# Last columns of an output projection: residual rows made one quarter of columns earlier, a part of the last norm on TensorE, the last block in 384 and 128 columns

## The chip, the cores and the metric

One core of a Trainium2 chip runs the whole kernel. The metric is device microseconds (us) of one execution; the figure quoted is the median of several executions.

## The reference, cut to what matters

Two layers over 512 latent tokens of 2048 features (and 256 context tokens, which only the first layer needs). The change touches the end of the second layer:

```
y_l   = sgu_mixer(xm_l, w_in_odd[j], ...)                 # 512 x 2048
x_lat = layer_norm(DEEPNORM_ALPHA * x_lat + g_l * (y_l @ w_out_odd[j]),
                   post_ln_g[layer], post_ln_b[layer])    # the output
```

`layer_norm` takes mean and variance over the 2048 features of a token, then multiplies by `post_ln_g` and adds `post_ln_b`. The `x_lat` on the right is the first layer's output. The kernel keeps it in DRAM without the first layer's factor and shift (`x1d`), so its residual rows are made when needed: `x1d * lng0 + lnb0`.

## The kernel before, in words

TensorE computes in fp32r, each operand split in a high and a low part: a product is three matmuls (high by high, high by low, low by high; lines 212 to 214). The parts of a weight are made by `split` (line 107): ScalarE casts the high part (L108), VectorE subtracts (L109).

The second output projection is one call of `out_phase` over four quarters of 512 columns, `out1`. In each quarter `form_b` runs over 16 blocks `kb` of the contraction, and for each over four blocks `t` of 128 tokens; the result of a `t` is one PSUM bank of 128x512. A quarter is 16 x 4 x 3 = 192 matmuls. The last quarter (c = 3) is called with `hold` = 16: token block t = 0 takes all 16 `kb` first, with the split weights kept in SBUF, then t = 1, 2 and 3 follow, each with 48 matmuls.

`evacuate` turns a finished bank into rows `z`: VectorE multiplies by the gate row (L1001), adds ALPHA times the residual rows (L1002) and takes statistics of the 512 columns (L1004). After the last quarter of a `t` the statistics are combined (L1051), EPS is added (L254), GpSimd takes the power -0.5 (L256), and `norm1` does, for each of four groups of 512 columns, a subtract-and-multiply (L1453), a multiply-and-add (L1454) and the DMA to `out` (L1455).

The residual rows: in the middle of a quarter (`n == KB // 2`) `ready` loads the two rows `lng0`, `lnb0`, broadcast to 128 partitions (L982, into a `pair_tile`), and the four 128x512 blocks of `x1d` (L1027, tag `t2`, four buffers). After that, one block per step, VectorE multiplies (L1033) and adds (L1034). The `pair_tile`s are four slots of 128x1024: slots 0 and 1 hold the gate rows of columns 0, 1 and 2, 3; slots 2 and 3 hold `lng0` and `lnb0` of even and of odd quarters.

The order of each engine's queue, the DMA issues on SyncE's queue included, is set when the kernel is built: a planner takes the program's instructions in order of priority (program order) as their inputs and buffers come free by its own times, so an instruction may stand ahead of its place in the text. `tc.issue_after(x)` puts the instructions in its block behind `x` on their engine. Everything then runs in that order.

Of the kernel before, what the change touches and what calls it, by code (L numbers as in the profile page):

```python
# [22 lines left out]
NH = 4  # L23
ALPHA = 4.0 ** 0.25
# [47 lines left out]
def tile_backbone(ctx: ExitStack, tc: tile.TileContext, io: dict, out: bass.AP):  # L72
    nc = tc.nc
    ve, sc, gp, te, dma = nc.vector, nc.scalar, nc.gpsimd, nc.tensor, nc.sync
    fl = Flow()

    big = ctx.enter_context(tc.tile_pool(name="big", bufs=1))
    wp = ctx.enter_context(tc.tile_pool(name="wp", bufs=1))
# [18 lines left out]
    ident = cst.tile([P, P], F32, tag="ident", name="ident")  # L97
# [45 lines left out]
    for c, _ in out1:  # L143
        stream += b_raws(io["woo"], c)
    raws, parts, used, newest, older = [], [], [0], [None], [None]


    AHEAD, HOLD = 2, 16
# [36 lines left out]
    def form_a(targets):  # L185

        for q in range(4):
# [13 lines left out]
                    te.matmul(pt[:, :n], b, xh_, start=False, stop=last)  # L201
            fl.pe(us)

    def form_b(tbs, stat, order, before=None, hold=0):


        pts = {t: ps() for t in tbs}
        ws = []

        def mm(t, n, kb, wh, wl):  # L210
            a, b = stat(kb, t)
            te.matmul(pts[t], a, wh, start=n == 0, stop=False)  # L212
            te.matmul(pts[t], a, wl, start=False, stop=False)  # L213
            te.matmul(pts[t], b, wh, start=False, stop=n == KB - 1)  # L214

        for n, kb in enumerate(order):
            if before is not None:
                before(n)
            ws.append(weights())
            now = tbs if n < KB - hold else tbs[:1]  # L220
            for t in now:
                mm(t, n, kb, *ws[n])
            fl.pe(3 * 0.216 * len(now))
        if not hold:
            yield pts
            return
        yield {tbs[0]: pts[tbs[0]]}
        for t in tbs[1:]:
            for n in range(KB - hold, KB):
                mm(t, n, order[n], *ws[n])  # L230
                fl.pe(3 * 0.216)
            yield {t: pts[t]}

    xh = [None] * KB
    xl = [None] * KB
# [61 lines left out]
    with ExitStack() as ev:  # L297
# [16 lines left out]
        rows = [[crow[k] for k in range(2)], [crows[:, k] for k in range(2)]]  # L314
# [32 lines left out]
        order = list(taken())  # L347
# [550 lines left out]
        for h in range(NH):  # L898
            qkv_tiles(h)
            ctx_in(h)  # L900
            early = h < 3
# [87 lines left out]

    def out_phase(seq, resid, gate, order, before, norm, finish, hold=0, affine=(), late=None):  # L990
        z = [la.tile([P, D], F32, tag=f"z{t}", name=nm("z")) for t in range(NT)]
        st = [la.tile([P, 4, 6], F32, tag=f"st{t}", name=nm("st")) for t in range(NT)]
        g = []

        evac, todo = [], []

        def evacuate(c, s, pts, xr):
            for n, t in enumerate(pts):
                if n and c < 3:
                    paced(z[t][:, s])  # L1000
                ve.tensor_tensor(z[t][:, s], pts[t], g[c], ALU.mult)  # L1001
                ve.scalar_tensor_tensor(z[t][:, s], xr[t], ALPHA, z[t][:, s], ALU.mult, ALU.add)  # L1002
                yield Y_E
                ve.bn_stats(st[t][:, c, :], z[t][:, s])  # L1004

        def product(c, tbs, before, hold, late):
            s = slice(c * 512, (c + 1) * 512)
            xr = {}

            def ready(n):  # L1010
                if before is not None:
                    before(n)
                if late is not None:
                    late(n)
                if n == KB // 2:
                    if not g:
                        gt = [pair_tile(i) for i in range(2)]
                        g.extend(half_row(gate, c_, gt[c_ // 2], c_ % 2) for c_ in range(4))
                    while evac:
                        fl.drain(evac.pop())  # L1020
                    rows = []
                    if affine:
                        rt = pair_tile(2 + c % 2)
                        rows = [half_row(a, c, rt, i) for i, a in enumerate(affine)]
                    for t in tbs:
                        xr[t] = la.tile([P, 512], F32, tag="t2", name=nm("xres"), bufs=4)
                        dma.dma_start(xr[t], resid[t * P:(t + 1) * P, s])  # L1027
                        if affine:
                            todo.append((xr[t], rows))
                if n > KB // 2 and todo:  # L1030

                    x_, rows = todo.pop(0)
                    ve.tensor_tensor(x_, x_, rows[0], ALU.mult)  # L1033
                    ve.tensor_tensor(x_, x_, rows[1], ALU.add)  # L1034

            for pts in form_b(tbs, y_stat, order, ready, hold):
                evac.append(fl.spawn(evacuate(c, s, pts, xr)))
                if c == 3:
                    fl.drain(evac.pop())
                yield pts  # L1040

        last = None
        for n, (c, tbs) in enumerate(seq):
            for pts in product(c, tbs, before if n == 0 else None, *((hold, late) if n == len(seq) - 1 else (0, None))):
                if c == 3:
                    if last is not None:
                        fl.drain(last)
                        last = None
                    for t in pts:
                        m2 = la.tile([P, 2], F32, tag="m2", name=nm("m2"), bufs=2)  # L1050
                        ve.bn_aggr(m2, st[t])  # L1051
# [59 lines left out]


    v = [None] * NT
    vst = [la.tile([P, 4, 6], F32, tag=f"st{t}", name=nm("vst")) for t in range(NT)]

# [218 lines left out]
    def spatial(q):  # L1334

        if q == 0:
            for t in range(NT):
                ve.bn_aggr(vm[t], vst[t])
# [234 lines left out]
```

## Time and profile before

| | |
|---|---|
| median of 3 runs | 1735.16 us (1733.09 to 1737.89) |
| the profiled execution | 1728.81 us, its span from first to last instruction 1726.9 us |
| mean granted TensorE clock | 0.997 of full speed |
| busy: TensorE, VectorE, ScalarE | 98%, 69%, 39% of the span |

How to read it: PE is the matmul side of TensorE and PEld its weight loads, DVE is VectorE, ACT ScalarE, POOL GpSimd, SP SyncE; SPq is SyncE's queue, which issues the DMAs. All places in time are us from the start of the span. A matmul's duration in a row contains the way through the array, so the pace of a stream is read from the distance of starts. Brackets at the end of a row give the idle time before it and what ended it.

### The profile page before, as it was taken

To read this page: it belongs to the slowest core of one execution; us is meant where nothing else is said; L and a number is where in the kernel's file an instruction comes from. 1 tells how busy PE (TensorE), PEld (TensorE's weight loads), DVE (VectorE), ACT (ScalarE), POOL (GpSimd) and SP (SyncE) were. 2 spreads that over 40 slices of the span, in tenths; PEclk is the share of its full clock that TensorE was granted. 3 is DMA by queue.
4 is the path that set the end of the run, shared out by engine and by line. 5 is a ranking of instruction groups with operands and counts; after the bars stand their busy time and mean duration, and the time that the engine had idled before them with its cause. 6 is when DMAs were issued, how large, how long until landed. Compare 5 with 4: busy or idle time off the path is not lost.

```text
span 1726.9 us, 22782 instructions
## 1 busy us (share of the span) xinstructions
PE 1700.4 (98%) x8260; PEld 1399.2 (81%) x8260; DVE 1200.2 (69%) x2133; ACT 681.8 (39%) x1176; POOL 75.1 (4%) x113
## 2 busy tenths in 40 slices
PE   8999999999999999999999999999999999999997
PEld 5777788888888888888888888877887888888885
DVE  5786486556798977866644477876876767665558
ACT  3223232323444445445432247634544354432230
POOL 0000000000000000000000000211110110000000
PEclk9999999999999999999999999999999999999998
DMA  8986277879687575663384567996767585765443
GB/s 316 375 333 254 83 244 241 278 268 316 226 279 273 202 250 173 213 197 123 111 261 138 147 225 263 214 275 168 217 166 221 134 242 137 208 168 166 131 143 113
DMA packets 143304, 366.63 MB, mean 212 GB/s; under 512 B 13526, under 2 KB 29870, under 8 KB 142678
## 3 DMA queue, kind: packets, MB, share of 16 engines
q1 hardware_dynamic: 127158, 324.79, 55.3%
q0 software_dynamic: 8640, 31.46, 10.3%
q10 hardware_dynamic: 7392, 8.91, 1.4%
q8 instruction: 65, 1.06, 0.2%
q14 instruction: 49, 0.40, 0.1%
HBM read 340.42 MB, written 24.69 MB: 211 GB/s over the span
## 4 chain that ended last, share of the span: by engine, by line
PE 96%; DMA 2%; DVE 1%; issue 0%; ACT 0%; DVEq 0%; SPq 0%; ACTq 0%
PE ps L212 11%; PE ps L214 11%; PE ps L213 11%; PE ps L1270 8%; PE ps L1271 8%; PE ps L1269 8%; PE ps L196 6%; PE ps L197 6%; PE ps L201 6%; PE ps L479 2%; PE ps L480 2%; PE ps L481 2%; PE ps L708 2%; DMA qr<-in_wq_dram 2%; PE ps L388 1%; PE ps L716 1%
## 5 line engine op out<-in xcount | busy, mean ns | idle before, releaser
L108 ACT CAST wh<-wr 128x512 fp32r<-128x512 f32 x328 | 201.1, 622 | 442.3 <-PE ps L214 260.9
L109 DVE TENSOR_TENSOR wh<-wr,wh 128x512 fp32r<-128x512 f32 x320 | 219.0, 687 | 202.0 <-ACT wh L108 200.3
L214 PE MATMUL ps<-wh,yl 128*128 128x512 f32 x512 | 199.5, 390 | 0.0
L212 PE MATMUL ps<-wh,yh 128*128 128x512 f32 x512 | 194.3, 391 | 0.0
L213 PE MATMUL ps<-wh,yh 128*128 128x512 f32 x480 | 187.0, 390 | 0.0
L196 PE MATMUL ps<-xh,wh 128*128 128x512 f32 x448 | 175.4, 392 | 0.0
L197 PE MATMUL ps<-xl,wh 128*128 128x512 f32 x448 | 175.0, 391 | 0.0
L201 PE MATMUL ps<-xh,wh 128*128 128x512 f32 x448 | 174.7, 390 | 0.0
L282 DVE SCALAR_TENSOR_TENSOR adw<-adw,crow 128x1024 f32<-128x1024 f32 x128 | 155.9, 1218 | 3.3 <-DMA adw<-in_adat_dram 3.3
L108 ACT CAST wh<-qr 128x1024 fp32r<-128x1024 f32 x96 | 101.1, 1058 | 138.0 <-DMA qr<-in_wq_dram 53.9
L1270 PE MATMUL ps<-wh,ch 128*128 128x512 f32 x384 | 149.8, 393 | 2.6 <-DVE wh L109 2.5
L1271 PE MATMUL ps<-wh,ch 128*128 128x512 f32 x384 | 149.0, 391 | 0.0
L1269 PE MATMUL ps<-wh,ch 128*128 128x512 f32 x384 | 143.5, 396 | 3.7 <-ACT wh L108 3.7
L109 DVE TENSOR_TENSOR wh<-qr,wh 128x1024 fp32r<-128x1024 f32 x96 | 116.6, 1221 | 28.9 <-PE ps L1270 12.8
L109 DVE TENSOR_TENSOR wh<-pair,wh 128x1024 fp32r<-128x1024 f32 x72 | 87.4, 1220 | 40.3 <-PE ps L1270 20.9
L1270 PE MATMUL ps<-wh,xn 128*128 128x512 f32 x288 | 112.6, 391 | 0.0
L1271 PE MATMUL ps<-wh,xn 128*128 128x512 f32 x288 | 112.5, 391 | 0.0
L214 PEld LDWEIGHTS ps<-wh,yl 128*128 128x128 f32 x512 | 96.1, 188 | 19.9
L212 PEld LDWEIGHTS ps<-wh,yh 128*128 128x128 f32 x512 | 96.0, 188 | 19.7
L1269 PE MATMUL ps<-wh,xn 128*128 128x512 f32 x288 | 107.6, 395 | 0.3 <-ACT wh L108 0.3
L213 PEld LDWEIGHTS ps<-wh,yh 128*128 128x128 f32 x480 | 90.2, 188 | 18.6
L108 ACT CAST wh<-pair 128x1024 fp32r<-128x1024 f32 x72 | 75.3, 1051 | 66.5 <-PE ps L1271 27.8
(320 smaller groups left out, 3281.5 us busy)
## 6 DMA issues: line engine op xcount, KB each, us to landing
adw<-in_adat_dram SPq DMA_DIRECT2D x128, 512.0 KB, 5.1
qr<-in_wq_dram SPq DMA_DIRECT2D x116, 512.0 KB, 4.8
wr<-in_wie_dram SPq DMA_DIRECT2D x60, 512.0 KB, 3.6
pair<-in_wq_dram POOLq DMA_DIRECT2D x56, 512.0 KB, 6.4
aw<-in_a_dram SPq DMA_DIRECT2D x52, 512.0 KB, 7.2
wr<-in_woe_dram SPq DMA_DIRECT2D x40, 512.0 KB, 4.5
wr<-in_woo_dram SPq DMA_DIRECT2D x32, 512.0 KB, 4.0
wr<-in_wv_dram SPq DMA_DIRECT2D x16, 512.0 KB, 5.4
```

Of the source, the lines that this page charges most:

```text
L108: sc.copy(hi, src)
L109: return ve.tensor_tensor(lo, src, f32(hi), ALU.subtract)
L196: te.matmul(pt[:, :n], a, xh_, start=first, stop=False)
L197: te.matmul(pt[:, :n], a, xl_, start=False, stop=False)
L201: te.matmul(pt[:, :n], b, xh_, start=False, stop=last)
L212: te.matmul(pts[t], a, wh, start=n == 0, stop=False)
L213: te.matmul(pts[t], a, wl, start=False, stop=False)
L214: te.matmul(pts[t], b, wh, start=False, stop=n == KB - 1)
L282: ve.scalar_tensor_tensor(ts[n], ts[n], 0.5, crow[k], ALU.mult, ALU.mult, accum_out=part[:, f % 4, k:k + 1])
L1269: te.matmul(pts[t], a, wh[:, s], start=first, stop=False, **more)
L1270: te.matmul(pts[t], a, wl[:, s], start=False, stop=False, **more)
L1271: te.matmul(pts[t], b, wh[:, s], start=False, stop=end, **more)
```

## The change

Three things, all in the second layer's last quarter of columns.

1. The residual rows of c = 3 are loaded and made in the third quarter (c = 2, from n = 13), into pair tiles 0 and 2, with `lng0`, `lnb0` in pair tile 3.
2. The last token block (t = 3) of c = 3 is computed as 384 and then 128 columns, each over all 16 `kb`, in two PSUM banks, and evacuated in these two parts (the statistics get a fifth group).
3. In the norm of t = 3, the multiply-and-add of the first 512 columns leaves VectorE: TensorE puts `lnb1` in a bank with a multiplication by the identity, adds diag(rstd) times the rows (plain fp32), and ScalarE copies the result back; ScalarE also makes diag(rstd). The four DMAs of t = 3 go out in the order 1, 2, 0, 3; for each `t` they stand behind its loop.

```
+    LAST = slice(0, 384), slice(384, 512)
     def form_b(tbs, stat, order, before=None, hold=0):
-        def mm(t, n, kb, wh, wl):
+        def mm(t, n, kb, wh, wl, s=slice(0, 512)):
             a, b = stat(kb, t)
...
+            te.matmul(pts[t][:, s], a, wh[:, s], start=n == 0, stop=False)
+            te.matmul(pts[t][:, s], a, wl[:, s], start=False, stop=False)
+            newest_mm[0] = te.matmul(pts[t][:, s], b, wh[:, s], start=False, stop=n == KB - 1)
...
         for t in tbs[1:]:
-            for n in range(KB - hold, KB):
-                mm(t, n, order[n], *ws[n])
-                fl.pe(3 * 0.216)
-            yield {t: pts[t]}
+            for s in (slice(0, 512),) if t != tbs[-1] else LAST:
+                if s.start:
+                    pts[t] = ps()
+                for n in range(KB):
+                    mm(t, n, order[n], *ws[n], s)
+                    fl.pe(3 * 0.000422 * (s.stop - s.start))
+                yield {t: pts[t]}
...
+        def evacuate(c, s, pts, xr, i=slice(0, 512)):
+            s = slice(s.start + i.start, s.start + i.stop)
...
+                ve.tensor_tensor(z[t][:, s], pts[t][:, i], g[c][:, i], ALU.mult)
+                ve.scalar_tensor_tensor(z[t][:, s], xr[t][:, i], ALPHA, z[t][:, s], ALU.mult, ALU.add)
                 yield Y_E
+                ve.bn_stats(st[t][:, n_st[t], :], z[t][:, s])
+                n_st[t] += 1
...
+                if hold and n == 0:
+                    xr.update(early)
+                if affine and c == 2 and n == KB - 3:
+                    rt, c_ = pair_tile(3), c + 1
+                    rows = [half_row(a, c_, rt, i) for i, a in enumerate(affine)]
+                    for i in (0, 2):
+                        x2 = pair_tile(i)
+                        for j in range(2):
+                            x_, t = x2[:, j * 512:(j + 1) * 512], i + j
+                            dma.dma_start(x_, resid[t * P:(t + 1) * P, c_ * 512:(c_ + 1) * 512])
+                            early[t] = x_
+                            todo.append((x_, rows))
-                if n == KB // 2:
+                if n == KB // 2 and hold:
+                    while evac:
+                        fl.drain(evac.pop())
+                elif n == KB // 2:
...
-                if n > KB // 2 and todo:
+                if (n > KB // 2 or hold) and todo:
...
     def norm1(t, z, m2, r_):
+        last = t == NT - 1
+        if last:
+            pt, dg = ps(), wp.tile([P, P], F32, tag="wraw", name="dg", bufs=3)
+            with tc.issue_after(newest_mm[0].ins):
+                te.matmul(pt, ident, lnr[1, 0], start=True, stop=False)
+            sc.activation(dg, ident, AF.Copy, scale=r_[:, 0:1])
         for c in range(4):
             s = slice(c * 512, (c + 1) * 512)
             ve.scalar_tensor_tensor(z[:, s], z[:, s], m2[:, 0:1], lnr[0, c], ALU.subtract, ALU.mult)
-            ve.scalar_tensor_tensor(z[:, s], z[:, s], r_[:, 0:1], lnr[1, c], ALU.mult, ALU.add)
+            if last and c == 0:
+                te.matmul(pt, dg, z[:, s], start=False, stop=True)
+                sc.copy(z[:, s], pt)
+            else:
+                ve.scalar_tensor_tensor(z[:, s], z[:, s], r_[:, 0:1], lnr[1, c], ALU.mult, ALU.add)
+        for c in (1, 2, 0, 3) if last else range(4):
+            s = slice(c * 512, (c + 1) * 512)
             dma.dma_start(out[t * P:(t + 1) * P, s], z[:, s])
```

## Rows read from the trace of the kernel before

**Rows 1.** The page: busy time of each engine with its share of the span, and the shares of the engines in the chain that ended last.

```profile
PE 1700.4 (98%) x8260; PEld 1399.2 (81%) x8260; DVE 1200.2 (69%) x2133; ACT 681.8 (39%) x1176; POOL 75.1 (4%) x113
...
PE 96%; DMA 2%; DVE 1%; issue 0%; ACT 0%; DVEq 0%; SPq 0%; ACTq 0%
```

**Rows 2.** Busy time by stretch: most of the third quarter of columns, then t = 0 and t = 3 of the last quarter. The columns are the stretch, its length, busy time of each engine (instructions), granted clock, share of the DMA engines, GB/s.

```profile
1640.00:1669.00 29.00, 29.00 (x129) 24.02 (x128) 13.32 (x21) 8.32 (x15) 0.00 (x0) 1.00 0.47 151
...
1671.40:1682.30 10.90, 10.90 (x50) 9.03 (x49) 8.54 (x18) 3.85 (x7) 0.00 (x0) 1.00 0.51 169
...
1704.10:1715.00 10.90, 10.85 (x48) 8.64 (x46) 10.09 (x18) 0.00 (x0) 0.92 (x1) 1.00 0.47 157
```

**Rows 3.** Instructions in order of time, PE, in t = 3 of the last quarter: two matmuls that stand 30 matmuls apart.

```profile
1707.31 0.39 PE L212 MATMUL ps<-wh,yh 128*128 128x512 f32 x1
...
1714.11 0.39 PE L212 MATMUL ps<-wh,yh 128*128 128x512 f32 x1
```

**Rows 4.** Instructions in order of time after TensorE's last matmul: DVE's (its L1002 and L1004 lie between the first two), and POOL's one.

```profile
1714.99 0.69 DVE L1001 TENSOR_TENSOR z<-ps,pair 128x512 f32<-128x512 f32 x1 [0.67 <-PE ps L214]
...
1717.17 0.26 DVE L1051 BATCH_NORM_AGGREGATE m<-st 128x2 f32<-128x24 f32 x1
1717.46 0.15 DVE L254 TENSOR_SCALAR vae<-m 128x1 f32<-128x1 f32 x1
1717.54 2.73 DVE L1453 SCALAR_TENSOR_TENSOR z<-z,m,lnr 128x512 f32<-128x512 f32 x4
1717.76 0.92 POOL L256 TENSOR_TENSOR rst<-vae,mhalf 128x1 f32<-128x1 f32 x1 [7.69 <-DVE vae L254]
1720.18 2.73 DVE L1454 SCALAR_TENSOR_TENSOR z<-z,rst,lnr 128x512 f32<-128x512 f32 x4
```

**Rows 5.** Half-microsecond stretches after the last matmul, columns as in rows 2: where the granted clock falls, and the first and last stretches in which the output's four last DMAs move data.

```profile
1716.50:1717.00 0.50, 0.00 (x0) 0.00 (x0) 0.50 (x1) 0.00 (x0) 0.00 (x0) 1.00 0.01 0
1717.00:1717.50 0.50, 0.00 (x0) 0.00 (x0) 0.43 (x3) 0.00 (x0) 0.00 (x0) 0.54 0.00 0
...
1721.40:1721.90 0.50, 0.00 (x0) 0.00 (x0) 0.50 (x2) 0.00 (x0) 0.00 (x0) 0.50 0.23 86
1721.90:1722.40 0.50, 0.00 (x0) 0.00 (x0) 0.50 (x2) 0.00 (x0) 0.00 (x0) 0.50 1.02 377
...
1724.40:1724.90 0.50, 0.00 (x0) 0.00 (x0) 0.00 (x0) 0.00 (x0) 0.00 (x0) 0.50 0.69 250
1724.90:1725.40 0.50, 0.00 (x0) 0.00 (x0) 0.00 (x0) 0.00 (x0) 0.00 (x0) 0.50 0.09 29
```

**Rows 6.** Instructions in order of time, PE: 18 matmuls of 256 columns in fp32r, each with its own 128x128 weights, in an earlier stage, and the second matmul after them.

```profile
448.36 2.30 PE L708 MATMUL ps<-qkv,aT 128*128 128x256 f32 x18
...
450.73 0.40 PE L213 MATMUL ps<-wh,xh 128*128 128x512 f32 x1
```

**Rows 7.** The same view: two matmuls of a single column, each with 128x128 weights, and the second matmul after them.

```profile
1402.77 0.28 PE L1360 MATMUL ps<-ones,wsp 128*128 128x1 f32 x2
...
1403.23 0.40 PE L1271 MATMUL ps<-wh,ch 128*128 128x512 f32 x1
```

**Rows 8.** The same view: 12 plain fp32 products of 128 columns, which the trace shows as 24 matmuls (two for each), with weights of 32x56, and the second matmul after them.

```profile
219.42 2.82 PE L608 MATMUL ps<-ga,sel 32*56 32x128 f32 x24
...
222.51 0.39 PE L480 MATMUL ps<-xl,wh 128*128 128x512 f32 x1
```

**Rows 9.** Groups by line and shape, DVE: instructions of 128 and of 256 columns.

```profile
L738 DVE TENSOR_TENSOR em<-es,kc 128x128 f32<-128x128 f32 x32 | 8.7, 288 | 18.9 <-DMA es<-ed 13.9 <-ACT w L739 4.9
...
L792 DVE BATCH_NORM_STATS2 st<-hg 128x6 f32<-128x256 f32 x16 | 6.7, 421 | 0.1
...
L770 DVE SCALAR_TENSOR_TENSOR w<-w,rd,w 128x128 f32<-128x128 f32 x16 | 5.6, 347 | 0.0
```

**Rows 10.** Nearest rows to the new work of the norm: ACT on 128x128, ACT's copy of a bank (groups by line and shape), and two plain fp32 products of 256 columns on PE (four matmuls) with the second matmul after them (in order of time).

```profile
L739 ACT ACTIVATE w<-em,bc 128x128 f32<-128x128 f32 x32 | 12.4, 393 | 0.0
...
L1280 ACT COPY qc<-ps 128x512 f32<-128x512 f32 x8 | 4.3, 583 | 0.0
...
1235.21 1.03 PE L1370 MATMUL ps<-v,wsp 128*128 128x256 f32 x4
...
1236.30 0.40 PE L1270 MATMUL ps<-wh,xn 128*128 128x512 f32 x1
```

**Rows 11.** Instructions in order of time, DVE, last quarter: the first evacuation of t = 0 and the end of the norm of t = 2.

```profile
1689.63 0.69 DVE L1001 TENSOR_TENSOR z<-ps,pair 128x512 f32<-128x512 f32 x1
...
1711.58 2.73 DVE L1454 SCALAR_TENSOR_TENSOR z<-z,rst,lnr 128x512 f32<-128x512 f32 x4
```

**Rows 12.** Instructions in order of time around the residual rows: DVE's last use of pair tile 3 in quarter 1, SyncE's next load into it; DVE's last use of pair tile 0 (quarter 1) and of pair tile 2 (quarter 2); DVE's first and last work on the residual rows of quarter 3.

```profile
1602.48 0.69 DVE L1034 TENSOR_TENSOR xres<-xres,pair 128x512 f32<-128x512 f32 x1
...
1603.20 0.33 SPq L982 DMA_DIRECT2D pair<-in_lng_dram  x1
...
1639.82 0.66 DVE L1001 TENSOR_TENSOR z<-ps,pair 128x512 f32<-128x512 f32 x1
...
1646.05 0.68 DVE L1034 TENSOR_TENSOR xres<-xres,pair 128x512 f32<-128x512 f32 x1
...
1678.64 0.67 DVE L1033 TENSOR_TENSOR xres<-xres,pair 128x512 f32<-128x512 f32 x1
...
1690.23 1.29 DVE L1034 TENSOR_TENSOR xres<-xres,pair 128x512 f32<-128x512 f32 x2
```

More of the change, by code (lines that the diff above doesn't have):

```diff
@@ L145, in tile_backbone @@
     raws, parts, used, newest, older = [], [], [0], [None], [None]
+    newest_mm = [None]
     AHEAD, HOLD = 2, 16
@@ L208, in form_b @@
         ws = []
-        def mm(t, n, kb, wh, wl):
+        def mm(t, n, kb, wh, wl, s=slice(0, 512)):
             a, b = stat(kb, t)
-            te.matmul(pts[t], a, wh, start=n == 0, stop=False)
-            te.matmul(pts[t], a, wl, start=False, stop=False)
-            te.matmul(pts[t], b, wh, start=False, stop=n == KB - 1)
+            te.matmul(pts[t][:, s], a, wh[:, s], start=n == 0, stop=False)
+            te.matmul(pts[t][:, s], a, wl[:, s], start=False, stop=False)
+            newest_mm[0] = te.matmul(pts[t][:, s], b, wh[:, s], start=False, stop=n == KB - 1)
         for n, kb in enumerate(order):
@@ L226, in form_b @@
             return
+        assert hold == KB
         yield {tbs[0]: pts[tbs[0]]}
         for t in tbs[1:]:
-            for n in range(KB - hold, KB):
-                mm(t, n, order[n], *ws[n])
-                fl.pe(3 * 0.216)
-            yield {t: pts[t]}
+            for s in (slice(0, 512),) if t != tbs[-1] else LAST:
[5 more added lines that the diff above has]
+                yield {t: pts[t]}
     xh = [None] * KB
@@ L991, in out_phase @@
         z = [la.tile([P, D], F32, tag=f"z{t}", name=nm("z")) for t in range(NT)]
[L992 to L997, printed above, removed]
+        st = [la.tile([P, 5, 6], F32, tag=f"st{t}", name=nm("st")) for t in range(NT)]
+        g, n_st = [], [0] * NT
+        evac, todo, early = [], [], {}
+        def evacuate(c, s, pts, xr, i=slice(0, 512)):
+            s = slice(s.start + i.start, s.start + i.stop)
             for n, t in enumerate(pts):
@@ L1000, in evacuate @@
                     paced(z[t][:, s])
-                ve.tensor_tensor(z[t][:, s], pts[t], g[c], ALU.mult)
-                ve.scalar_tensor_tensor(z[t][:, s], xr[t], ALPHA, z[t][:, s], ALU.mult, ALU.add)
+                ve.tensor_tensor(z[t][:, s], pts[t][:, i], g[c][:, i], ALU.mult)
+                ve.scalar_tensor_tensor(z[t][:, s], xr[t][:, i], ALPHA, z[t][:, s], ALU.mult, ALU.add)
                 yield Y_E
-                ve.bn_stats(st[t][:, c, :], z[t][:, s])
+                ve.bn_stats(st[t][:, n_st[t], :], z[t][:, s])
+                n_st[t] += 1
         def product(c, tbs, before, hold, late):
@@ L1034, in ready @@
                     ve.tensor_tensor(x_, x_, rows[1], ALU.add)
-            for pts in form_b(tbs, y_stat, order, ready, hold):
-                evac.append(fl.spawn(evacuate(c, s, pts, xr)))
+            for n, pts in enumerate(form_b(tbs, y_stat, order, ready, hold)):
+                parts_ = LAST if hold and n >= NT - 1 else (slice(0, 512),)
+                evac.append(fl.spawn(evacuate(c, s, pts, xr, parts_[n - NT + 1] if len(parts_) > 1 else parts_[0])))
                 if c == 3:
                     fl.drain(evac.pop())
-                yield pts
+                if len(parts_) == 1 or n == NT:
+                    yield pts
         last = None
@@ L1050, in out_phase @@
                         m2 = la.tile([P, 2], F32, tag="m2", name=nm("m2"), bufs=2)
-                        ve.bn_aggr(m2, st[t])
+                        ve.bn_aggr(m2, st[t][:, 0:n_st[t], :])
                         norm(t, z[t], m2, rstd_of(la, m2[:, 1:2], 1))
@@ L1113, in tile_backbone @@
     v = [None] * NT
-    vst = [la.tile([P, 4, 6], F32, tag=f"st{t}", name=nm("vst")) for t in range(NT)]
+    vst = [la.tile([P, 5, 6], F32, tag=f"st{t}", name=nm("vst")) for t in range(NT)]
     comb = {}
@@ L1337, in spatial @@
             for t in range(NT):
-                ve.bn_aggr(vm[t], vst[t])
+                ve.bn_aggr(vm[t], vst[t][:, 0:4, :])
                 r_ = rstd_of(la, vm[t][:, 1:2], 1)
```

## The prediction

> **What bounds the kernel now.** I read the page first: TensorE is busy 98% of the span and 96% of the chain that ended last [rows 1]. In the second output projection, TensorE is busy 29.00 of 29.00 us in the third quarter of columns and 10.90 of 10.90 in t = 0 of the last, where weights, splits and residual rows all meet [rows 2]. So nothing that comes earlier for VectorE or the DMAs can pull TensorE's end forward: only fewer or shorter matmuls can, or a shorter tail behind the last one.
>
> The tail came next, from the instructions in order of time. VectorE starts on the last bank at 1714.99, having waited 0.67 us for TensorE [rows 4]; I set TensorE's end at 1714.96. Then VectorE works without a hole: evacuation to 1717.17 (three steps of 0.73), statistics to 1717.54, four subtractions to 1720.18 (0.66 each), four multiply-adds to 1722.91. GpSimd's power fits beside it (1717.76 to 1718.68). The data of the last four DMAs (4 x 128 x 512 x 4 bytes = 1.05 MB) moves from about 1721.8 to 1724.95 at up to 377 GB/s and a share of 1.02 of the DMA engines [rows 5]: from its first byte this stream is as long as its bytes take, 3.17 us, and VectorE's last multiply-adds aren't what it waits for. The span ends 1.95 us after it. So the tail is: first multiply-add done (1720.18 + 0.69 = 1720.87), 0.91 until data moves, 3.17 of stream, 1.95 to the end.
>
> **The change part by part.**
>
> *Residual rows earlier.* Eight VectorE instructions leave the last quarter (first at 1678.64, last pair at 1690.23 [rows 12]). They are why VectorE reaches t = 0 at 1689.63 [rows 11], 7.3 us after that bank is done: TensorE's end less three blocks of 48 x 0.2267 = 10.88 gives 1682.3. They return in the third quarter, where VectorE is busy 13.32 of 29.00 us [rows 2]: 8 x 0.6 = 4.8 us fit. The DMAs are four of 256 KB, moved and not added, plus two row loads that already went out early: SyncE loaded pair tile 3 at 1603.20, as soon as its last reader was done at 1603.17 [rows 12], a whole quarter ahead of the text. By the same habit the new loads go out when pair tile 0 (1640.48) and pair tile 2 (1646.73) fall free, when the DMA engines are at a share of 0.47 [rows 2]. Queued behind them on SyncE are the weight loads; a free buffer means no wait, so only the bytes count: 1.05 MB at some 0.33 MB/us [rows 5] is 3.2 us of transfer inside 29 us half empty. On the path: 0. Bounds: 0, and 3.2 us if every byte delayed a weight that TensorE then awaited. A gain isn't possible here: in before VectorE is done with t = 2 at 1714.31 [rows 11], 0.67 us ahead of the last bank.
>
> *384 and 128 columns.* This is the term that decides. Before, t = 3 is 48 matmuls of 512 columns; (1714.11 − 1707.31) / 30 = 0.2267 us each [rows 3], 10.88 in all. After, it is 48 of 384 and 48 of 128, each matmul still with its own 128x128 weights. For 256 columns the pace is (450.73 − 0.227 − 448.36) / 18 = 0.119 [rows 6] (I count to the second matmul after the stretch and take off one of 0.227, as the first is started early). Between 512 and 256 that is 0.42 ns a column, so 384 columns take 0.173: 8.30 us. For 128 the same line gives 0.065. But the trace has shorter matmuls and they are not faster: one column with 128x128 weights takes (1403.23 − 0.227 − 1402.77) / 2 = 0.117 [rows 7], and 128 columns of plain fp32 (222.51 − 0.227 − 219.42) / 24 = 0.119 [rows 8]. With one column there is nothing to stream, so 0.117 is what the change of weights takes. I take 0.117: 48 x 0.117 = 5.62 us. Together 13.92 instead of 10.88: **+3.04**. Bounds for the 128 columns: 0.065 (loads hidden entirely; 3.12 us, so +0.54) and 0.238 (the pair of rows 8: fp32r at this width as dear as a plain fp32 product; 11.42 us, so +8.84).
>
> *Evacuation of 128 columns.* TensorE ends at 1718.00. The 384 columns are ready 5.62 us earlier, at 1712.4; VectorE, 4.8 us ahead of before, is done with t = 2 by then, and their three steps (under 2.2 us) hide behind the 128. Even without the early residual rows VectorE would be free at 1714.31 and done at 1716.5. What is left on the path is three steps on 128 columns: 0.288 and 0.347 [rows 9], the statistics 0.29 by the line through 0.421 for 256 columns and 0.69 for 512; with the gap of 0.03 seen in rows 4 some 0.32 each. So 1718.03 + 0.96 = 1718.99, and with L1051 and L254 as before (0.37; a fifth group adds a few hundredths) the subtractions start at 1719.36.
>
> *The norm.* The four subtractions stay ahead of the multiply-adds (they don't need the power): to 1722.00. The first multiply-add, now of columns 1, ends at 1722.69; the others at 1723.35 and 1724.01, one fewer than before. TensorE's part: power done 0.30 + 0.92 us after L254 ends, at 1720.7; ScalarE's diagonal 0.39 [rows 10]; then one plain fp32 product of 512 columns: four matmuls of 256 took (1236.30 − 0.227 − 1235.21) = 0.86 [rows 10], the same columns twice over, so 0.86 plus 0.17 through the array, or 1.9 if the clock is at half (before, it falls from 1.00 to 0.54 at 1717.0, some 2 us after TensorE stopped [rows 5]; here the product with the identity ends near 1718.9 and the next starts at 1721.1); ScalarE's copy 0.58. Done at 1722.8 to 1723.7. Its DMA is third, behind one that waits for 1723.35, so at worst it is 0.3 us late while the stream still has two blocks to move. Cost 0; without that cover, the 0.3.
>
> *Stream and end.* Data from 1722.69 + 0.91 = 1723.60, 3.17 us, to 1726.77; later blocks come every 0.66 us and are ahead of the stream's 0.79 a block. Plus 1.95: 1728.72. Span +1.8 us: TensorE +3.04, evacuation −1.22; the multiply-add taken from VectorE earns nothing, because the first of them, not the last, starts the stream.
>
> **The rivals.**
>
> *Loads hidden.* If a 128-column matmul hides its weight load as the 512-column one does, it takes 0.065: TensorE ends at 1715.5 and the whole at −0.7 us, 1734.5. For it: only that PEld runs beside PE all the time; against it rows 7 and 8. The Trainium skill, page "TensorE: Matmul & The Clock Gate", section "Back-to-back issue gap", gives a sustained pace of about 81 ns for pairs of load and matmul at 128 columns and 131 ns at 512. The trace does not agree at 512, where it shows 227; by 81 ns the 128 columns would be 3.89 us and the kernel +0.1. Chance 0.17.
>
> *Narrow fp32r at the price of plain fp32* (the other side). No row shows fp32r under 256 columns. If it is run there in two passes, as rows 8 are, 48 x 0.238 = 11.42 us: TensorE +8.84, tail −1.22, +7.6 us, 1742.8. It decides above 0.17 us a matmul, where the sum passes 0.3%. For it: the change from 256 to fewer is untested; against it: L708's 0.119 is already at the floor, so nothing asks for a second pass. Chance 0.20.
>
> *Weights late.* The moved loads push a weight and TensorE waits up to 3.2 us more: 1740.2. Against it: a share of 0.47. Chance 0.06.
>
> *The early rows do nothing.* That they are off the path is already in my sum; it would only show with hidden loads, when VectorE without them would come 1.0 us late (1716.5 against 1715.5).
>
> **How the numbers follow.** The sum is made against the profiled execution, 1728.81 us (span 1726.9): 1730.6 there. That execution lies 6.3 us under the median of the three runs, so I put the difference on the median: 1735.16 + 1.8 = 1737.0, chance 0.57. The likeliest case's own range is 1734 to 1740 (the runs differ by ±2.4 us). Leaving out little of the cases on either side, hidden loads less that spread and plain-fp32 price, the range is 1732.0 to 1743.3. About 0.3%, 5.2 us, is what a measurement of this kernel tells from no change. Slower by more: most of the 0.20, half of the weights case, a few hundredths of the likeliest: 0.23. Faster by more: nothing in the profile gives it, since the tail shrinks by 1.2 us and the rest is TensorE at full pace: 0.03. Same: 0.74.
>
> **What would show it.** The distance of starts among the 128-column matmuls: 0.117, with PEld busy throughout (0.065 or 0.24 for the rivals); TensorE's last matmul of the projection near 1718; L1001 on 128 columns right after it, with an idle time before it; three L1454 after four L1453; L1033 and L1034 of the last quarter between 1641 and 1669; the last four DMAs still one unbroken stream. I am wrong if the 128-column pace is elsewhere, if the granted clock falls in the narrow stretch, or if TensorE has a hole between 1640 and 1704.

## The result, and the profile after

The changed kernel took 1736.79 us (median of 14 runs); the kernel before, timed beside it, 1733.09 us. The ratio is 1.0025 with a 95% interval of 1.0015 to 1.0036, so the change costs 4.3 us (2.6 to 6.2; the two medians lie 3.7 us apart). The whole interval lies above zero: the change is slower, by its middle by a little less than the 0.3% that the prediction took for the smallest difference that can be told. The forecast was +1.8 us.

The profiled executions differ by more than the change does (spans 1726.9 and 1735.1 us), because executions differ before the changed stretch is reached. Up to the middle of the third quarter every engine's queue holds the same instructions in the same order in both kernels. So I compare the two traces from a common event on, in three stretches:

- A: from the first matmuls of the third quarter (taken as 2.06 us after VectorE's first evacuation of quarter 1) to the first matmul of t = 3 in the last quarter;
- B: from there to VectorE's first instruction on the last bank;
- C: from there to the end of the span. Spans are printed to a tenth, so C is good to about 0.05 us.

| | A | B | C | sum against before |
|---|---|---|---|---|
| before | 75.94 | 11.08 | 11.91 | |
| after | 78.64 | 13.85 | 10.80 | +2.70 +2.77 −1.11 = +4.36 |

The sum, +4.36, agrees with the timing. The forecast had 0, +3.04 and −1.22. The miss lies in A.

**Stretch B, the narrow matmuls.** Instructions of PE in order of time (start, duration, engine, line, operation, tiles, shapes); L216 to L218 are L212 to L214 of before. First the ends of the 384 columns, then the ends of the 128 columns, then the norm's product with diag(rstd):

```profile
1710.45 0.33 PE L216 MATMUL ps<-wh,yh 128*128 128x384 f32 x1
...
1718.62 0.33 PE L218 MATMUL ps<-wh,yl 128*128 128x384 f32 x1
...
1718.96 0.27 PE L218 MATMUL ps<-wh,yl 128*128 128x128 f32 x1
...
1723.99 0.28 PE L218 MATMUL ps<-wh,yl 128*128 128x128 f32 x1
...
1727.30 1.13 PE L1491 MATMUL ps<-z,dg 128*128 128x512 f32 x2 [2.13 <-ACT dg L1486]
```

The first and last of the 384 columns are 47 matmuls apart: 8.17/47 = 0.174 us each. The two L218 of 128 columns are 45 apart: 5.03/45 = 0.112. A third of the columns costs two thirds of the time, as the narrow matmuls of [rows 7, 8] had it. TensorE was busy without a hole in that stretch, at full clock, so this is its pace and no wait; its weight loads (the second busy time) fill the stretch too, where [rows 2] have 24.02 of 29.00 us:

```profile
1722.60:1724.30 1.70, 1.70 (x16) 1.70 (x16) 0.00 (x0) 0.00 (x0) 0.00 (x0) 1.00 0.00 0
```

(Stretch and length, then busy time of PE, PEld, DVE, ACT, POOL with their instructions, granted clock, share of the DMA engines, GB/s, as in [rows 2].)

**Stretch C, the tail.** DVE's and ACT's instructions in order of time, against [rows 4]:

```profile
1718.99 0.56 DVE L1011 TENSOR_TENSOR z<-ps,pair 128x384 f32<-128x384 f32 x1 [0.42 <-PE ps L218]
...
1724.30 0.29 DVE L1011 TENSOR_TENSOR z<-ps,pair 128x128 f32<-128x128 f32 x1 [3.56 <-PE ps L218]
...
1725.28 0.29 DVE L1080 BATCH_NORM_AGGREGATE m<-st 128x2 f32<-128x30 f32 x1
...
1725.67 2.73 DVE L1489 SCALAR_TENSOR_TENSOR z<-z,m,lnr 128x512 f32<-128x512 f32 x4
1728.32 2.07 DVE L1494 SCALAR_TENSOR_TENSOR z<-z,rst,lnr 128x512 f32<-128x512 f32 x3
...
1728.47 0.59 ACT L1492 COPY z<-ps 128x512 f32<-128x512 f32 x1 [1.22 <-PE ps L1491]
```

From the evacuation's start to the first subtraction it takes 1.37 us, against 2.55 in [rows 4]. The first multiply-add ends at 1728.32 + 0.69 = 1729.01, ScalarE's copy of the product at 1728.47 + 0.59 = 1729.06. Which of them starts the stream of the last DMAs? SyncE's queue (its first issue of the four, and its wait before it: us in total, times, longest):

```profile
1729.08 0.33 SPq L1497 DMA_DIRECT2D out_dram<-z  x1
...
SPq L1497 <- ACT z L1492: 10.1, 1, 10.1
```

It is the copy. The text of the kernel has the order 1, 2, 0, 3, but the order of the queue is the planner's, and there the block that TensorE and ScalarE make goes first. Here it was ready at the same time as the first multiply-add's block, so it cost nothing. From there on the data moves as one stream (half-microsecond windows, columns as above; all windows of the stream together move 1.05 MB):

```profile
1729.50:1730.00 0.50, 0.00 (x0) 0.00 (x0) 0.50 (x2) 0.00 (x0) 0.00 (x0) 0.50 0.13 53
1730.00:1730.50 0.50, 0.00 (x0) 0.00 (x0) 0.39 (x1) 0.00 (x0) 0.00 (x0) 0.50 1.00 381
```

The stream's last data moves at about 1733.1. VectorE's last multiply-add ends at 1730.39, some 2.7 us before that.

**Stretch A, the miss.** TensorE waited in a stretch where the kernel before has no wait of TensorE at all:

```profile
1673.03 0.50 PE L217 MATMUL ps<-wh,yh 128*128 128x512 f32 x1 [0.26 <-DVE wh L109]
...
1680.15 0.50 PE L216 MATMUL ps<-wh,yh 128*128 128x512 f32 x1 [0.21 <-ACT wh L108]
1681.64 0.50 PE L217 MATMUL ps<-wh,yh 128*128 128x512 f32 x1 [0.98 <-DVE wh L109]
```

The bracket is the idle time ahead of an instruction and what ended it: a split of a weight, each time. The three sum to 1.45 us, but a hole costs more than its idle time: by the distance of starts, which is 0.227 elsewhere, TensorE lost 2.67 of the 2.70 us from 1672.39 to 1685.03, over 44 matmuls. (0.31 of it belongs to a fourth late start, at 1684.69, before which the engine was idle for only 0.04 us.)

The cause stands 20 us earlier. VectorE's instructions where the early residual rows (L1060, L1061; tile `pair` for t = 0 to 3 of c = 3) meet the splits (L109):

```profile
1656.27 0.62 ACT L108 CAST wh<-wr 128x512 fp32r<-128x512 f32 x1 [2.10 <-PE ps L218]
```

```profile
1657.06 0.69 DVE L1060 TENSOR_TENSOR pair<-pair,pair 128x512 f32<-128x512 f32 x1 [2.56 <-DMA pair<-x1d]
1658.16 0.69 DVE L1060 TENSOR_TENSOR pair<-pair,pair 128x512 f32<-128x512 f32 x1 [0.40 <-DMA pair<-x1d]
1658.77 1.28 DVE L1061 TENSOR_TENSOR pair<-pair,pair 128x512 f32<-128x512 f32 x2
1659.97 1.29 DVE L109 TENSOR_TENSOR wh<-wr,wh 128x512 fp32r<-128x512 f32 x2
```

ScalarE's cast was done at 1656.89, so the subtraction could have run then. It ran at 1659.97, 3.1 us later: ahead of it in VectorE's queue stood four instructions on residual rows, the first of which waited 2.56 us for its DMA. Only when this subtraction is done is the raw weights' buffer (`wr`) free, and a weight load in SyncE's queue waits for it. SyncE's queue (its lines, then its waits between 1640 and 1670):

```profile
1653.33 0.79 SPq L1036 DMA_DIRECT2D pair<-x1d  x2
1654.22 0.38 SPq L170 DMA_DIRECT2D wr<-in_woo_dram  x1
1660.68 0.38 SPq L170 DMA_DIRECT2D wr<-in_woo_dram  x1
...
SPq L170 <- DVE wh L109: 15.3, 5, 6.0
...
SPq L1036 <- DVE xres L1061: 4.9, 1, 4.9
```

From the common event on (3.84 us apart in the two traces) the loads at 1654.22 and 1660.68 stand at 1650.38 and 1656.84 of before's time, where the same two loads of before stand 3.0 and 5.8 us earlier:

```profile
1647.36 0.38 SPq L169 DMA_DIRECT2D wr<-in_woo_dram  x1
...
1651.08 0.37 SPq L169 DMA_DIRECT2D wr<-in_woo_dram  x1
```

The load at 1660.68 goes out as soon as the late subtraction is done (1659.97 + 0.69 = 1660.66). The last line of the waits shows a second suspect: SyncE itself stood 4.9 us at an early row's load, waiting for pair tile 2, and the load at 1654.22 stands right behind that. And the loads' 1.05 MB is a third. The experiments take these apart.

### The profile page after: what moved, and what is told of

It is laid out like the page before. It is cut to its first block, busy times and chain, and to the rows that moved or that the text cites. A ratio compares the mean times of both kernels' runs of the same rounds, so it can differ in the third digit from the quotient of the medians.

```text
span 1735.1 us, 22890 instructions
## 1 busy us (share of the span) xinstructions
PE 1709.3 (99%) x8312; PEld 1404.9 (81%) x8312; DVE 1200.2 (69%) x2135; ACT 682.5 (39%) x1178; POOL 74.9 (4%) x113
## 4 chain that ended last, share of the span: by engine, by line
PE 86%; DMA 8%; DVE 4%; issue 1%; ACT 1%; DVEq 0%; SPq 0%; ACTq 0%
PE ps L217 10%; PE ps L218 10%; PE ps L216 10%; PE ps L1299 7%; PE ps L1300 7%; PE ps L1298 7%; PE ps L197 6%; PE ps L198 6%; PE ps L202 6%; DMA qr<-in_wq_dram 4%; PE ps L488 2%; PE ps L489 2%; PE ps L490 2%; PE ps L717 2%; DVE wh L109 2%; PE ps L397 1%
## 5 line engine op out<-in xcount | busy, mean ns | idle before, releaser
L109 DVE TENSOR_TENSOR wh<-wr,wh 128x512 fp32r<-128x512 f32 x320 | 218.4, 687 | 197.6 <-ACT wh L108 196.2
L218 PE MATMUL ps<-wh,yl 128*128 128x512 f32 (+2 forms) x528 | 202.9, 385 | 0.0
L216 PE MATMUL ps<-wh,yh 128*128 128x512 f32 (+2 forms) x528 | 197.9, 386 | 0.2 <-ACT wh L108 0.2
L217 PE MATMUL ps<-wh,yh 128*128 128x512 f32 (+2 forms) x488 | 189.2, 388 | 1.3 <-DVE wh L109 1.2
L109 DVE TENSOR_TENSOR wh<-qr,wh 128x1024 fp32r<-128x1024 f32 x96 | 116.6, 1220 | 28.8 <-PE ps L1299 15.0
L216 PEld LDWEIGHTS ps<-wh,yh 128*128 128x128 f32 x528 | 99.0, 188 | 20.0 <-ACT wh L108 0.6
L109 DVE TENSOR_TENSOR wh<-pair,wh 128x1024 fp32r<-128x1024 f32 x72 | 87.5, 1220 | 39.8 <-PE ps L1299 20.0
L218 PEld LDWEIGHTS ps<-wh,yl 128*128 128x128 f32 x528 | 99.2, 188 | 19.1
L217 PEld LDWEIGHTS ps<-wh,yh 128*128 128x128 f32 x488 | 91.7, 188 | 20.6 <-DVE wh L109 2.4
```

What stands on the lines that cost most here:

```text
L109: return ve.tensor_tensor(lo, src, f32(hi), ALU.subtract)
L216: te.matmul(pts[t][:, s], a, wh[:, s], start=n == 0, stop=False)
L217: te.matmul(pts[t][:, s], a, wl[:, s], start=False, stop=False)
L218: newest_mm[0] = te.matmul(pts[t][:, s], b, wh[:, s], start=False, stop=n == KB - 1)
```

## The experiments

All are compared in the stretches A, B and C; where a ratio stands, it is to the kernel before on the same chip, with its 95% interval. The ratios alone don't part most of the versions, as their intervals overlap. What carries the argument on A is the traces, one for each version: 75.93 or 75.94 in six of the seven that have no early row work ahead of the splits (before among them), 76.26 in the seventh, and 77.8 to 82.6 in the four that have it.

**The early residual rows alone.** The last block in one piece, the norm as before:

```diff
-    LAST = slice(0, 384), slice(384, 512)
+    LAST = slice(0, 512),
...
-        last = t == NT - 1
+        last = False
```

> Only the first part: the residual rows of the last quarter are made during the third quarter; the last block is one of 512 columns and the norm is VectorE's alone. Three stretches of the profile are read: A from the second matmul of the third quarter to the first matmul of t = 3 of the last (75.93 us before, 78.64 after), B from there to VectorE's first instruction on the last bank (11.08 before, 13.85 after), C from there to the end of the span (11.91 before, 10.80 after). If the late weights come from this part alone: A 78.6, B 11.1, C 11.9, some 2.7 us (0.16%) slower than before. Rival, that A grew through the run's own spread: A 75.9, the same as before.

Measured: A 78.2, B 11.08, C 11.98; ratio 1.0010 (0.9999 to 1.0022), 1735.44 us. TensorE waits twice for a split, 1.2 us, as in the whole change. So the early rows by themselves lengthen A, by 2.3 us in the trace, and give nothing back.

**All but the early rows.**

```diff
-                if affine and c == 2 and n == KB - 3:
+                if False:
...
-                if n == KB // 2 and hold:
+                if False:
...
-                if (n > KB // 2 or hold) and todo:
+                if n > KB // 2 and todo:
```

> The whole change without its first part (residual rows where they were). If the first part alone makes the weights late: A 75.9, B 13.85, C 10.8, some 1.7 us (0.1%) slower than before. If the early rows were needed so that VectorE is free for the 384 columns, C is longer than 10.8 or the statistics of the 384 columns end after TensorE's last matmul; I expect them to end some 1.5 us before it. Rival, that A grew for another reason: A 78.6.

Measured: A 75.93, B 13.86, C 10.83: +1.7 us by the stretches, the forecast's sum to 0.1 us. The timed ratio is 1.0022 (1.0012 to 1.0031), or +3.8 us (2.1 to 5.4), whose lower end lies just above the trace's 1.7. What makes that difference stays open, and with it how much of A's 2.70 us the timing of the whole change (+4.3) holds. Were the early rows needed for the split block? VectorE's instructions say no:

```profile
1717.33 0.55 DVE L1011 TENSOR_TENSOR z<-ps,pair 128x384 f32<-128x384 f32 x1
...
1721.17 0.29 DVE L1011 TENSOR_TENSOR z<-ps,pair 128x128 f32<-128x128 f32 x1 [2.10 <-PE ps L218]
```

Three steps of 0.56 from 1717.33 on, and the 384 columns are evacuated; VectorE then waits 2.10 us for the 128.

**The early rows' loads on GpSimd's queue** instead of SyncE's, so that SyncE doesn't stand at them:

```diff
-                            dma.dma_start(x_, resid[t * P:(t + 1) * P, c_ * 512:(c_ + 1) * 512])
+                            gp.dma_start(x_, resid[t * P:(t + 1) * P, c_ * 512:(c_ + 1) * 512])
```

> The whole change, but GpSimd's queue instead of SyncE's issues the four loads of the early residual rows; the bytes are the same, and VectorE still makes the rows in the third quarter. Theory one, the loads in SyncE's queue wait for pair tile 2 and hold the weight loads behind them: A falls back to 75.9 to 76.5. Theory two, the 1 MB takes the DMA engines' time from the weights: A stays 78 or more. Theory three, VectorE's work on the rows stands ahead of the splits of weights in its queue: A stays between, 77 or more.

Measured: A 82.59, C 11.53; ratio 1.0049 (1.0034 to 1.0065), 1740.48 us. The wait of SyncE is gone and A grew by another 4 us, so TensorE loses time without that wait too. VectorE's queue, TensorE's largest hole, and a window behind it:

```profile
1657.85 0.69 DVE L1060 TENSOR_TENSOR pair<-pair,pair 128x512 f32<-128x512 f32 x1 [4.51 <-DMA pair<-x1d]
1658.46 0.68 DVE L109 TENSOR_TENSOR wh<-wr,wh 128x512 fp32r<-128x512 f32 x1
...
1683.74 0.50 PE L216 MATMUL ps<-wh,yh 128*128 128x512 f32 x1 [2.67 <-ACT wh L108]
...
1685.50:1688.00 2.50, 2.50 (x7) 1.94 (x6) 2.50 (x7) 0.00 (x0) 0.00 (x0) 0.50 0.67 216
```

The rows' data came later, VectorE stood still for it 4.51 us instead of 2.56, and the splits stood behind it. Not all of the growth is that: after the hole of 2.67 us the granted clock fell to 0.50, and seven distances of starts in a row were 0.427 instead of 0.227, which is 1.4 us.

C is longer here too, 11.53 against 10.80. The reason is the order of the last DMAs:

```profile
1730.79 2.07 DVE L1494 SCALAR_TENSOR_TENSOR z<-z,rst,lnr 128x512 f32<-128x512 f32 x3
...
1731.88 0.59 ACT L1492 COPY z<-ps 128x512 f32<-128x512 f32 x1 [2.17 <-PE ps L1491]
...
1732.49 0.33 SPq L1497 DMA_DIRECT2D out_dram<-z  x1
```

The norm's product ran at half clock in this execution (2.08 us instead of 1.13). The first multiply-add was done at 1731.48, but SyncE's first issue of the four stood until the copy's end at 1732.47: with the copy's block first in the queue, the product is on the path.

**The rows in tiles that are free already:** t = 2 in another, idle buffer and t = 3 loaded later, so that no load waits for pair tile 2.

```diff
-                    for i in (0, 2):
-                        x2 = pair_tile(i)
-                        for j in range(2):
-                            x_, t = x2[:, j * 512:(j + 1) * 512], i + j
+                    x2 = pair_tile(0)
+                    xm = la.tile([P, 512], F32, tag="mx", name=nm("xm"))
+                    for t, x_ in enumerate((x2[:, 0:512], x2[:, 512:1024], xm)):
...
+                    xr[3] = la.tile([P, 512], F32, tag="t2", name=nm("xres"), bufs=4)
+                    dma.dma_start(xr[3], resid[3 * P:4 * P, s])
```

> The whole change, but pair tile 2 isn't used: the block of t = 2 goes to a tile that has long been free, that of t = 3 is loaded and made in the last quarter as before; tokens 0 and 1 stay in pair tile 0. Three quarters of the bytes are still early and in SyncE's queue, and none of them waits for pair tile 2. Theory one (the wait for pair tile 2): A 75.9 to 76.3. Theory two (bytes): A about 78. Theory three (VectorE's order): A about 77.5.

Measured: A 77.83, B 13.85, C 10.80; ratio 1.0024 (1.0008 to 1.0039). Still 1.9 us in A, with less work moved than was meant: the planner put the row of t = 2 further ahead still (its load at 1535.4, its work at 1616.9 and 1618.6, before A), so that only t = 0 and 1, four instructions and half of the bytes, are left in the third quarter. VectorE no longer stands still for data there, but does the row work first and then three splits in one go, and TensorE waits once, some 29 us on:

```profile
1658.03 0.69 DVE L1064 TENSOR_TENSOR xres<-xres,pair 128x512 f32<-128x512 f32 x1
1658.63 1.90 DVE L109 TENSOR_TENSOR wh<-wr,wh 128x512 fp32r<-128x512 f32 x3
...
1687.26 0.50 PE L216 MATMUL ps<-wh,yh 128*128 128x512 f32 x1 [1.59 <-ACT wh L108]
```

**The same loads, the row work behind the splits.** Loads, tiles and bytes stay as in the change; only VectorE's two instructions per row are held behind the newest split:

```diff
-                    ve.tensor_tensor(x_, x_, rows[0], ALU.mult)
-                    ve.tensor_tensor(x_, x_, rows[1], ALU.add)
+                    with tc.issue_after(newest[0].ins) if any(x_ is e for e in early.values()) else nullcontext():
+                        ve.tensor_tensor(x_, x_, rows[0], ALU.mult)
+                        ve.tensor_tensor(x_, x_, rows[1], ALU.add)
```

> The whole change, with the loads of the early residual rows as they are in SyncE's queue, but VectorE's work on these rows is placed behind the split of weights that was planned last when it is written, so that it no longer stands ahead of the splits of the third quarter. Theory three (the row work, waiting for its loads in VectorE's queue, holds the splits of weights behind it, these the buffers, and these the next weight loads): A 75.9 to 77. Theory one (the loads wait for pair tile 2 in SyncE's queue): they wait a little less, as pair tile 2 falls free earlier, and A stays at 78 or more only if this wait is what counts. Theory two (bytes): 78 or more.

Measured: A 75.94, B 13.85, C 10.78; ratio 1.0017 (1.0006 to 1.0027), 1734.79 us. A is that of the kernel before to the last digit, and TensorE has no wait. Yet all four loads still go out early, with all their bytes, and SyncE still stands at one of them (first line, a wait of SyncE's queue; it was 4.9 us), with the next weight loads behind it. VectorE's splits now wait for ScalarE's cast alone, and the rows follow at 1667:

```profile
SPq L1036 <- DVE xres L1062: 2.7, 1, 2.7
...
1651.94 0.38 SPq L170 DMA_DIRECT2D wr<-in_woo_dram  x1
...
1655.14 0.38 SPq L170 DMA_DIRECT2D wr<-in_woo_dram  x1
```

```profile
1654.42 0.69 DVE L109 TENSOR_TENSOR wh<-wr,wh 128x512 fp32r<-128x512 f32 x1 [2.03 <-ACT wh L108]
...
1667.20 0.68 DVE L1061 TENSOR_TENSOR pair<-pair,pair 128x512 f32<-128x512 f32 x1
```

By the common event (4.06 us apart) the two weight loads that were 3.0 and 5.8 us late are now 0.5 and 0.0 us late. That settles A: it isn't the bytes, but the place of the row work in VectorE's queue. SyncE's wait hangs on the same place: pair tile 2 falls free only when VectorE has done the third quarter's own last row, so row work ahead of that lengthens the wait, and the 2.7 us that are left of it cost nothing. How much of the 2.70 us went by that wait and how much by the splits directly isn't parted; without the wait and with half of the row work it was 1.9.

**448 and 64 columns** (without the early rows), to see whether the pace has a floor:

```diff
-    LAST = slice(0, 384), slice(384, 512)
+    LAST = slice(0, 448), slice(448, 512)
```

> The change without early residual rows (A 75.9), the last block as 448 and 64 columns. If the change of weights sets the pace of the narrow matmuls: 0.112 us a matmul at 64 columns as at 128, and 0.200 at 448, so B = 48 x 0.312 = 15.0. If a narrow matmul costs by its columns: 0.056 to 0.065, B 12.4 to 12.9. C some 0.5 shorter than with 128 columns: 10.3.

Measured in one run: A 75.94, B 15.69, C 10.88. The instructions of 64 columns, from their first L218 to the turn, and the windows there:

```profile
1718.29 0.28 PE L218 MATMUL ps<-wh,yl 128*128 128x64 f32 x1
...
1722.76 0.28 PE L216 MATMUL ps<-wh,yh 128*128 128x64 f32 x1
...
1723.04 0.40 PE L218 MATMUL ps<-wh,yl 128*128 128x64 f32 x1
```

```profile
1720.50:1722.50 2.00, 2.00 (x20) 2.00 (x19) 0.00 (x0) 0.00 (x0) 0.00 (x0) 1.00 0.03 8
1722.50:1723.00 0.50, 0.50 (x6) 0.50 (x6) 0.00 (x0) 0.00 (x0) 0.00 (x0) 0.93 0.00 0
1723.00:1723.50 0.50, 0.50 (x5) 0.50 (x4) 0.00 (x0) 0.00 (x0) 0.00 (x0) 0.50 0.00 0
```

From 1718.29 to 1722.76 the pace is 4.47/40 = 0.112, that of 128 columns: half the columns buy nothing. Then the granted clock falls to 0.50, the lower of its two levels, with TensorE busy 0.50 of 0.50 us, and the last matmuls come every 0.21. The evacuation up to the first subtraction is 0.19 us shorter (1.18 against 1.37), but C isn't: the norm's product ran at half clock too, 2.08 us instead of 1.13, ScalarE's copy ended at 1729.63, a microsecond after the first multiply-add (1728.64), and SyncE's queue, which has the copy's block second in this version, stood 0.5 us for it.

**TensorE's part of the norm alone:** no early rows, the last block in one piece.

```diff
-    LAST = slice(0, 384), slice(384, 512)
+    LAST = slice(0, 512),
...
-                if affine and c == 2 and n == KB - 3:
+                if False:
...
```

> The third part alone: TensorE makes a part of the last norm, one block of 512 columns, residual rows where they were. A 75.9, B 11.1. If the end hangs on the first finished block, because the stream of the four DMAs is as long as its bytes take: C 11.9, no gain. If it hangs on VectorE's last multiply-add: C 11.25, a gain of 0.66.

Measured in one run: A 75.94, B 11.08, C 11.96 against 11.91. The multiply-add taken from VectorE earns nothing. The stream is as unbroken as before; its second window, at full rate:

```profile
1728.00:1728.50 0.50, 0.00 (x0) 0.00 (x0) 0.40 (x1) 0.00 (x0) 0.00 (x0) 0.50 1.01 385
```

**A version to beat both: 256 and 256 columns, the norm in another order,** so that the first block is ready two subtractions sooner (no early rows):

```diff
-    LAST = slice(0, 384), slice(384, 512)
+    LAST = slice(0, 256), slice(256, 512)
...
+        sub(0)
+        sub(1)
...
+        for c in range(1 if last and True else 0, 4):
+            m = mul(c)
+            nxt = c + 1 if last and True else c + 2
+            if nxt < 4:
+                with tc.issue_after(m.ins) if last else nullcontext():
+                    sub(nxt)
...
```

The other token blocks' norms get two subtractions ahead of the first multiply-add too.

> A version that may beat both: no early residual rows; the last block as 256 and 256 columns (48 x 2 x 0.119 = 11.42 instead of 10.88); in the norms VectorE's order is subtract 0, subtract 1, then multiply-add and subtract in turns, so that the first block is finished after three instructions instead of five; TensorE's part of the norm stays. If the end hangs on the first finished block: A 75.9, B 11.6, C 10.3 (evacuation 0.86 shorter, first block 1.3 earlier, of which the stream's holes take back 0.5): 1.1 us (0.06%) faster than before, which a ratio hardly tells from no change. If it hangs on the last multiply-add: C 10.4 to 10.6 too, but with the stream ending right after it; told apart by the 0.5 us stretches of DMA traffic.

Measured: ratio 1.0001 (0.9993 to 1.0010): no different from before, and better than the change. A 76.26, B 11.71, C 10.68 instead of the 10.3 hoped for. The stream starts sooner, and then has to wait, for ScalarE's copy (0.7 us in SyncE's queue) and for VectorE, which makes a block every 1.4 us:

```profile
1727.50:1728.00 0.50, 0.00 (x0) 0.00 (x0) 0.50 (x1) 0.38 (x1) 0.00 (x0) 0.95 0.72 283
1728.00:1728.50 0.50, 0.00 (x0) 0.00 (x0) 0.50 (x2) 0.00 (x0) 0.00 (x0) 0.50 0.63 242
```

**That order of the norm alone,** on the last block in one piece; all else, the order in the other token blocks too, is as in the run before:

```diff
-    LAST = slice(0, 256), slice(256, 512)
+    LAST = slice(0, 512),
```

> Only the norm of the last token block differs from the kernel before: TensorE makes its first 512 columns, and VectorE's order is subtract 0, subtract 1, multiply-add 1, subtract 2, multiply-add 2, subtract 3, multiply-add 3, so that the first of the last DMAs may start two subtractions (1.3 us) sooner. No early residual rows, no split of the block. Theory: the last DMAs then wait for VectorE, which has a block ready only every 1.4 us, as in the run with 256 and 256 columns, where the span ended 8.9 us after the first subtraction; before, the first subtraction came 2.55 us after VectorE started on the last bank, so the end comes 2.55 + 8.9 = 11.45 us after that start instead of 11.91: 0.46 us shorter. Rival: the stream is as long as its bytes from the first byte on, 3.17 us, and starts 1.3 us sooner: 10.6 us. The stretch of the earlier blocks is 75.94 and the last block's matmuls 11.08 us by both, if the 0.3 us longer first stretch of the 256 and 256 run came with the split; 76.2 if it came with the order of the norm. Ratio to the kernel before 0.9997 by the theory, which timing can't tell from no change; the profile can.

Measured: ratio 1.0004 (0.9993 to 1.0014). A + B is that of before (87.02), so the 0.3 us by which A was longer with 256 and 256 columns doesn't come from the norm's order. In that trace one weight load, issued at the same place as here to 0.1 us, was ready for ScalarE's cast 0.7 us later (1675.56 against 1670.05, common events 4.79 apart), so that its buffer, the next load and then one matmul were late; why the load took longer stays open. C is 12.23, which neither theory expected: longer than before. The product with diag(rstd) took 2.07 us here, ScalarE's copy ended at 1723.85, and SyncE's queue had that block's DMA second; it waited 1.7 us for the copy, and the block behind it had been ready since 1723.22. So the run says nothing against the order itself: in the run of TensorE's norm alone the same product took 1.13. The stream stops (until 1724.5):

```profile
1723.50:1724.00 0.50, 0.00 (x0) 0.00 (x0) 0.47 (x2) 0.35 (x1) 0.00 (x0) 0.50 0.00 0
```

## Why the prediction was right, and where it was not

The time fell inside the range and on the side of the forecast, but the change cost 2.5 us more than the sum. That the absolute figures agree so well, 1737.0 forecast and 1736.79 measured, is luck: the base of three runs, 1735.16, lay 2.1 us above the 1733.09 of the fourteen, which made up for most of the miss. By its steps:

- **128 columns: right.** Forecast 0.117 us a matmul, from the row of a single column; measured 0.112. With 0.174 for 384 columns (forecast 0.173), B grew by 2.77 instead of 3.04. The 64 columns confirm that below some width the pace no longer goes by the columns. That the change of weights is what sets it fits the weight loads, busy 1.70 of 1.70 us, but is argued: every narrow matmul in these runs has new weights, so a fixed cost of another kind for each matmul isn't excluded.
- **The rivals on that pace: both wrong.** Loads hidden would have been 0.065 and plain fp32's price 0.238. The Trainium skill, page "TensorE: Matmul & The Clock Gate", section "Back-to-back issue gap", has about 81 ns at 128 columns; this trace has 112. (The bound at which the second rival decides is misread in the prediction: its sum passes 0.3% at 0.19 us a matmul, not at 0.17.)
- **Evacuation: right.** Forecast −1.22. From its start to the first subtraction it measured 1.37 instead of 2.55, −1.18; the fifth group of statistics makes up 0.03 of the difference (L1080 took 0.29, against 0.26 for L1051 of before).
- **The norm on TensorE: 0 as forecast, but by luck.** The step rested on the product's block being third in the queue, with at most 0.3 us to lose. It is first: SyncE's long wait ahead of the stream (10.1 us) ended with ScalarE's copy, at 1729.06, 0.05 us after the first multiply-add. The step did reckon with a half clock, and in this trace the clock held; where the product ran at half clock in the same order (the run with GpSimd's queue), C was 0.73 us longer. It also put the power's start 0.30 us behind the end of L254, where [rows 4] have that distance from its start.
- **Early residual rows: wrong.** The step said "a free buffer means no wait, so only the bytes count", and put 0. Measured: +2.70 in A, with holes of TensorE where the prediction said that a hole would prove it wrong. The size is near the bound of the rival "Weights late" (3.2, chance 0.06), but that bound was the time of the bytes, and the run that kept every byte and every load, with VectorE's row work behind the splits, has nothing of it. The step counted VectorE's eight instructions as 4.8 us that fit into a stretch with room (13.32 of 29.00 busy), and didn't ask what stands behind them in VectorE's queue. It also took pair tile 2 to be free at 1646.73, which is 1650.57 on the changed trace's clock; its load went out at 1653.33, when its last reader, work on the third quarter's own rows in the same queue, had ended (1652.62 + 0.69). The chain is: row work, some of it waiting for its DMA, stands ahead of splits; raw weights' buffers come free late; the next weight loads go out 3 to 6 us late; and some 20 us later TensorE has used up its lead.
- **What the early rows were worth: right, nothing.** Without them the 384 columns were evacuated 2.10 us before the 128 were ready.

So by the traces the change is the sum of a trade that loses 1.7 us (narrow matmuls cost 2.77, C gives 1.11 back) and a move that loses 2.7.

## What to carry to other kernels

Work moved into a stretch where an engine is half idle isn't free because it fits: look at what stands behind it in that engine's in-order queue, above all when the moved instruction waits for a DMA and the next one frees a buffer that feeds the bound engine. To shorten a tail by cutting the last block of matmuls, price the narrow piece by the trace's narrowest matmuls and not by its columns. And where the end is a stream of DMAs, find what starts it and whether it breaks; a faster last step behind its start earns nothing. Read which transfer is first from the queue and not from the program's text.

## What the runs showed of the hardware

- With weights of 128x128 changed at every matmul, fp32r took 0.227 us for 512 columns, 0.174 for 384, 0.12 for 256, 0.112 for 128 and 0.112 for 64, at full clock.
- The granted clock fell from 1.00 to 0.50 in the midst of 64-column matmuls, with TensorE busy all the time (1722.5 to 1723.0); in the 128-column matmuls of the changed kernel it stayed at 1.00. The norm's product took 2.08 us at the lower level instead of 1.13.
- A hole of TensorE cost more than its idle time: with four late starts and 1.49 us of idle time before them, the starts were put back by 2.67 us. The matmul behind a hole is part of it: the next one starts 0.34 us after it instead of 0.227.
